# A hybrid RWKV-7 and band-attention encoder on one core: two slots of small steps in a row, then eight steps of large products

## The chip, the cores and the metric

The kernel runs on one core of a Trainium2 chip. A core has five engines that run their own queues in parallel and meet through semaphores: TensorE (PE, matrix products into PSUM), VectorE (DVE) and ScalarE (ACT) for elementwise work, GpSimd (POOL), and SyncE (SP), which here only issues DMAs. Each engine takes its instructions in the order in which they stand in its queue. The metric is the device time of one execution in microseconds (us), as the median of several runs; lower is better.

## What is computed

The reference is a trunk of two layers on 256 tokens of width 2048. Layer 0 mixes over time with RWKV-7 and then has a squared-ReLU MLP; layer 1 attends in bands of chunks and has another such MLP. The change touches only the time mixing, which the reference writes as a recurrence over the tokens for each of 32 heads of size 64:

```python
r = xr @ w_r
k = xk @ w_k
v = xv @ w_v
...
def step(S, inp):
    r_t, w_t, k_t, v_t, kk_t, a_t = inp
    sa = jnp.einsum('bhvk,bhk->bhv', S, -kk_t)
    S = (S * w_t[:, :, None, :] + sa[..., None] * (kk_t * a_t)[:, :, None, :]
         + v_t[..., None] * k_t[:, :, None, :])
    y = jnp.einsum('bhvk,bhk->bhv', S, r_t)
    return S, y
...
y = y.reshape(B, T, D).astype(h.dtype) * g
return y @ w_o
```

## The kernel before

Everything is held feature by token: 16 tiles of 128 features by 256 tokens. A large product is made of two parts for accuracy. The weight and the activation are each split into a high and a low half in a rounded 32-bit format (`halves` for weights: ACT casts a 128x1024 tile to `wH` in line 378, DVE subtracts to get `wL` in line 381; there are three buffers of each). One step over a tile of 128 inputs (one "kt") is two matmuls, line 412 (wH by both halves of the activation, 512 columns) and line 413 (wL by the high half, 256 columns). A projected tile takes 16 such kt. One pair of `wH` and `wL` covers eight kt.

The time mixing works on 16 pairs of heads (128 features each), one `Pair` object for each. The scan over the tokens is turned into four chunks of 64 tokens. A pair goes through 36 small steps, written as a generator that yields after each:

- `early`, steps 0 to 7: decay, learning rate, normalised key, all elementwise but for a few matmuls (lines 127 and 128 at step 0, the head sums of line 115 at steps 2 and 7, line 105 at step 6). DVE's line 154 at step 3 is the reader of the head sums of step 2.
- `invert`, steps 8 to 19: a triangular inverse for all chunks at once. Step 8 multiplies keys (line 105 into `gr`), ACT copies the parts `da` and `co`, POOL masks them. Step 9 is 16 small transposes by matmul. Steps 10 to 19 are five levels of two: the even one multiplies `tt` by `al` or `co` (line 111) and ACT copies the product to `xs` (lines 243 and 248); the odd one multiplies `u` by `xs` (line 111 again), DVE adds it to `u` (line 254, at the last level line 258 as well) and transposes `u` to `tt` (line 239). The odd step of a level cannot start before ACT has copied `xs`.
- `late`, steps 20 to 35: the four chunks one after the other, three steps each (lines 280 to 307; ACT copies `g` and `sa`, DVE makes the state `zs`), then the normalisation (the head sums of line 115 at step 33, ACT lines 318 and 319, DVE line 320) and the output gate (two matmuls in line 324 at step 35).

The scratch PSUM of the small steps (`psm`, tile `ms`) has two buffers that are handed out in turn, so a third user waits until the reader of the first is through.

The loop over slots (line 871) interleaves the pairs. Pair j starts at slot 8(j+1) and takes one step in each slot, so in the steady part four or five pairs are alive at once, eight steps apart. In every slot the small steps are issued first (inverting pairs, then late ones, then early ones), and after them the large products ("dense"): up to slot 127 two yields of `proj_steps`, that is four kt of the key or receptance projection of the pair that starts next; from slot 128 to slot 163, when all projections are done, the first part of the output projection (`out_steps`, 44 yields of two kt spread evenly over the 36 slots). `issue_after(last)` keeps PE's instructions of a block behind the last one recorded before. In three of four slots from slot 16 on, `ada()` adds one tile of another product, which DVE does by itself (line 454).

The order on PE is thus small steps, four kt, small steps, four kt, and so on. The order on the other engines is chosen by a scheduler from the recorded instructions; they do not follow `issue_after`. A period below is eight slots: one new pair, 32 kt.

Of the kernel before, what the change touches and what calls it, by code (L numbers as in the profile page):

```python
# [24 lines left out]
NPAIR = D // P  # L25
# [304 lines left out]
class Body:  # L330
# [299 lines left out]
    def layer_a(self, st, sp):  # L630
        nc, tc, d = self.nc, self.tc, self.d
# [5 lines left out]
        with ExitStack() as s1:  # L637
# [123 lines left out]
            for n in range(KT):  # L761
# [12 lines left out]
                first, last = n == 0, n == KT - 1  # L774
# [40 lines left out]
        with ExitStack() as s1:  # L815
            pw = self.pw = s1.enter_context(tc.tile_pool(name="pw", bufs=1, reuse_waits="tile"))
            pp = self.pp = sp.enter_context(tc.tile_pool(name="ps_b", bufs=1, space=bass.MemoryType.PSUM,
                                                         reuse_waits="tile"))
            self.psm = lambda: pp.tile([P, 512], F32, tag="ms", bufs=2, name="ms")
            e01 = [pw.tile([P, 4, C + 1], F32, name=f"e01_{i}") for i in range(2)]  # L820
            self.uf = [pw.tile([P, 4, C], F32, name=f"uf_{i}") for i in range(2)]
            for e, u in zip(e01, self.uf):
                nc.vector.memset(e[:, :, 0:1], 1.0)
                nc.gpsimd.memset(u, 0.0)

            pairs = [Pair(self, j, v[:, j, :], tw, ta, tg, e01[j % 2]) for j in range(NPAIR)]

            def proj_steps(pr):
                for dst, hl in (("k", xk), ("r", xr)):
                    w = self.wnext  # L830
                    src = next(weights, None)
                    self.wnext = None if src is None else self.weight(src)
                    ps = pp.tile([P, 2, T], F32, tag="pj", bufs=2, name="pj")
                    for kt in range(KT):
                        self.proj2(ps, w, lambda kt: hl[:, kt, :, 0:T], (kt, kt + 1))
                        if dst == "r" and kt == 1:
                            pr.lw = pw.tile([96, 2, P], F32, tag="lw", bufs=1, name="lw")
                            nc.sync.dma_start(out=pr.lw, in_=d["lora2"][pr.j, :96, 0:2])
                        if kt % 2 == 1:
                            if kt == KT - 1:  # L840
                                t = pw.tile([P, T], F32, tag=dst, bufs=2, name=dst)
                                nc.scalar.copy(t, ps[:, 0, :])
                                nc.vector.tensor_tensor(out=t, in0=ps[:, 1, :], in1=t, op=ALU.add)
                                setattr(pr, dst, t)
                            yield

            def out_steps():

                for n in range(8):
                    self.split(self.y_hl, n, v[:, n, :])  # L850
                sums, todo = self.o_ps, [(n, 0, HK) for n in range(8)] + [(n, HK, KT - 2) for n in range(4)]
                for n, lo, hi in todo:
                    if n % 2 == 0 and lo == 0:
                        tag = ("pj", "pj", "gr", "iv")[n // 2]
                        ps = pp.tile([P, 2 * T], F32, tag=tag, bufs=1 + (tag == "pj"), name="o")
                        sums.append(ps.rearrange("p (i t) -> p i t", i=2))
                    if lo == HK and n == 0:
                        assert all(p.done for p in pairs[:KT - 2])
                        for j in range(HK, KT - 2):
                            self.split(self.y_hl, j, v[:, j, :])  # L860
                    w = self.weight_part(d["w_o"][n], lo, hi)
                    for kt in range(lo, hi, 2):
                        self.proj(sums[n // 2][:, n % 2, :], w, lambda kt: self.y_hl[:, kt, :, 0:T],
                                  (kt, kt + 2), n % 2 == 0, False)
                        yield

            self.o_ps = []
            S, OUTS = self.SLOTS, 44
            inverts = range(Pair.EARLY, Pair.EARLY + Pair.INVERT)
            outs, done, n_out = None, 0, 0  # L870
            for slot in range(S * NPAIR + Pair.STEPS):
                live = []
                for j, pr in enumerate(pairs):
                    at = slot - S * (j + 1)
                    if 0 <= at < Pair.STEPS:
                        if at == 0:
                            pr.gen = pr.steps()
                        live.append((0 if at in inverts else 1 + (at < Pair.EARLY), -at, pr))
                        pr.done = at == Pair.STEPS - 1
                last = self.last_pe()  # L880
                for _, _, pr in sorted(live, key=lambda x: x[:2]):
                    with tc.issue_after(last):
                        next(pr.gen)
                    last = self.last_pe()
                if slot < S * NPAIR:
                    if slot % S == 0:
                        dense = proj_steps(pairs[slot // S])
                    todo = 16 // S
                else:
                    if outs is None:  # L890
                        self.y_hl = self.new_hl()
                        outs = dense = out_steps()
                    todo = OUTS * (slot + 1 - S * NPAIR) // Pair.STEPS - n_out
                    n_out += todo
                with tc.issue_after(last):
                    for _ in range(todo):
                        next(dense, None)
                if slot >= 2 * S and slot % 4 < 3:
                    self.ada()
            self.fin(HK)  # L900
# [306 lines left out]
```

## Time and profile before

| what | value |
|---|---|
| median of 3 runs (lowest, highest) | 2672.63 us (2672.55, 2673.03) |
| the profiled execution | 2673.81 us, of which its span is 2672.0 us |
| busy share of the span | PE 97%, PE weight loads 83%, DVE 79%, ACT 50%, POOL 8% |
| instructions | PE 23690 matmuls, DVE 3109, ACT 2432, POOL 320 |
| first projected key tile to last, of 16 (DVE line 843) | 216.8 us to 621.4 us |
| start of the last projected receptance tile's sum | 633.1 us |
| mean granted TensorE clock | 0.994 of full speed |

The page gives each engine's busy time; a row of a timeline gives the start in us, the duration, the engine, the line, what is written and what is read, and how many instructions were merged into it (for the small matmuls two for each line of the kernel that issues one). A bracket at the end of a row gives the idle time of the engine before it and the instruction whose end released it. The duration of a matmul contains its way through the array, so that successive matmuls overlap in these rows: what a matmul costs PE is the distance between starts. The time mixing's slots lie between about 209 and 715 us of the span; the two MLPs and the attention follow.

### The profile page before, as it was taken

To read this page: it belongs to the slowest core of one execution; us is meant where nothing else is said; L and a number is where in the kernel's file an instruction comes from. 1 tells how busy PE (TensorE), PEld (TensorE's weight loads), DVE (VectorE), ACT (ScalarE), POOL (GpSimd) and SP (SyncE) were. 2 spreads that over 40 slices of the span, in tenths; PEclk is the share of its full clock that TensorE was granted. 3 is DMA by queue.
4 is the path that set the end of the run, shared out by engine and by line. 5 is a ranking of instruction groups with operands and counts; after the bars stand their busy time and mean duration, and the time that the engine had idled before them with its cause. 6 is when DMAs were issued, how large, how long until landed. Compare 5 with 4: busy or idle time off the path is not lost. (4 is left out here: it accounts for less than half of the span.)

```text
span 2672.0 us, 58365 instructions
## 1 busy us (share of the span) xinstructions
PE 2600.1 (97%) x23690; PEld 2225.4 (83%) x23690; DVE 2101.0 (79%) x3109; ACT 1343.9 (50%) x2432; POOL 209.7 (8%) x320
## 2 busy tenths in 40 slices
PE   6999999999999999999999999999999999999997
PEld 3777788788899888888888998877898888888886
DVE  5778888889789888888888898899887556555555
ACT  3345555555456445355365554565564463453554
POOL 0001322332110000000000100000100000000002
PEclk9999999999999999999999999999999999999999
DMA  9966556565768888899898679887766555555553
GB/s 337 314 236 211 192 173 210 189 206 195 245 240 304 324 309 321 322 324 331 320 328 294 238 240 325 324 274 259 264 216 237 186 187 188 189 186 185 189 189 119
DMA packets 217390, 662.64 MB, mean 248 GB/s; under 512 B 21408, under 2 KB 68896, under 8 KB 217120
## 3 DMA queue, kind: packets, MB, share of 16 engines
q1 hardware_dynamic: 215056, 656.36, 71.1%
q8 instruction: 186, 3.05, 0.5%
q10 hardware_dynamic: 2064, 2.54, 0.3%
q14 instruction: 84, 0.69, 0.1%
HBM read 656.72 MB, written 2.10 MB: 247 GB/s over the span
## 5 line engine op out<-in xcount | busy, mean ns | idle before, releaser
L381 DVE TENSOR_TENSOR wL<-raw,wH 128x1024 fp32r<-128x1024 f32 x772 | 940.9, 1220 | 342.6 <-ACT wH L378 337.8
L378 ACT CAST wH<-raw 128x1024 fp32r<-128x1024 f32 x772 | 805.5, 1045 | 801.2 <-PE pj L412 646.0
L412 PE MATMUL pj<-aHL,wH 128*128 128x512 f32 x3328 | 1201.9, 403 | 2.0 <-DVE x L927 1.1
L413 PE MATMUL pj<-aHL,wL 128*128 128x256 f32 x3328 | 936.3, 281 | 0.0
L412 PEld LDWEIGHTS pj<-aHL,wH 128*128 128x128 f32 x3328 | 629.5, 189 | 154.1 <-issue 9.2
L412 PE MATMUL pj<-hHL,wH 128*128 128x512 f32 x2048 | 724.6, 399 | 0.0
L413 PEld LDWEIGHTS pj<-aHL,wL 128*128 128x128 f32 x3328 | 629.7, 189 | 2.6 <-issue 0.8
L413 PE MATMUL pj<-hHL,wL 128*128 128x256 f32 x2048 | 574.7, 281 | 0.0
L412 PEld LDWEIGHTS pj<-hHL,wH 128*128 128x128 f32 x2048 | 384.8, 188 | 95.7 <-DVE hHL L973 0.2
L413 PEld LDWEIGHTS pj<-hHL,wL 128*128 128x128 f32 x2048 | 387.0, 189 | 0.1
L454 DVE SCALAR_TENSOR_TENSOR acc<-rada,ct,acc 128x1024 f32<-128x1024 f32 x256 | 327.5, 1279 | 8.4 <-DMA rada<-w_ada 7.5
L518 POOL TENSOR_TENSOR ss<-ss,sq 128x256 f32<-128x256 f32 x56 | 54.5, 974 | 1590.8 <-ACT sq L517 1590.5
L998 DVE SCALAR_TENSOR_TENSOR x<-pj,mod,x 128x256 f32<-128x256 f32 x256 | 123.3, 482 | 59.5 <-PE pj L413 55.7
L454 DVE SCALAR_TENSOR_TENSOR acc<-raw,ct,acc 128x1024 f32<-128x1024 f32 x104 | 136.4, 1312 | 15.5 <-DMA raw<-w_ada 15.4
L401 PE MATMUL pj<-aHL,wH 128*128 128x258 f32 x384 | 109.0, 284 | 0.0
L402 PE MATMUL pj<-aHL,wH 128*128 128x258 f32 x384 | 109.0, 284 | 0.0
L970 ACT ACTIVATE t<-t 128x256 f32<-128x256 f32 x112 | 46.8, 418 | 122.6 <-DVE t L942 122.6
L403 PE MATMUL pj<-aHL,wL 128*128 128x258 f32 x384 | 108.0, 281 | 0.0
L403 PEld LDWEIGHTS pj<-aHL,wL 128*128 128x128 f32 x384 | 73.2, 191 | 0.2
L402 PEld LDWEIGHTS pj<-aHL,wH 128*128 128x128 f32 x384 | 72.6, 189 | 0.1
L401 PEld LDWEIGHTS pj<-aHL,wH 128*128 128x128 f32 x384 | 72.2, 188 | 0.2
L972 ACT ACTIVATE t<-t 128x256 f32<-128x256 f32 x128 | 53.4, 417 | 3.4
(244 smaller groups left out, 2812.3 us busy)
## 6 DMA issues: line engine op xcount, KB each, us to landing
raw<-w_up SPq DMA_DIRECT2D x256, 512.0 KB, 4.1
raw<-w_down SPq DMA_DIRECT2D x256, 512.0 KB, 4.1
rada<-w_ada SPq DMA_DIRECT2D x209, 512.0 KB, 5.7
raw<-w_ada SPq DMA_DIRECT2D x111, 512.0 KB, 4.4
rawa<-w_ada SPq DMA_DIRECT2D x64, 512.0 KB, 6.8
rada<-w_ada_kv SPq DMA_DIRECT2D x64, 512.0 KB, 6.6
raw<-w_k SPq DMA_DIRECT2D x32, 512.0 KB, 4.2
raw<-w_r SPq DMA_DIRECT2D x32, 512.0 KB, 4.5
```

The lines of the kernel that those rows point to most:

```text
L378: nc.scalar.copy(Hf, raw)
L381: eng.tensor_tensor(out=Lf, in0=raw, in1=Hf, op=ALU.subtract)
L401: nc.tensor.matmul(ps, H[:, i, :], a(kt)[:, 0, :], start=(first and kt == 0), stop=False)
L402: nc.tensor.matmul(ps, H[:, i, :], a(kt)[:, 1, :], start=False, stop=False)
L403: ins = nc.tensor.matmul(ps, L[:, i, :], a(kt)[:, 0, :], start=False, stop=(last and kt == KT - 1))
L412: nc.tensor.matmul(ps, H[:, i, :], a(kt), start=(kt == 0), stop=False)
L413: ins = nc.tensor.matmul(ps[:, 0, :], L[:, i, :], a(kt)[:, 0, :], start=False, stop=(kt == KT - 1))
L454: nc.vector.scalar_tensor_tensor(out=self.acc, in0=raw, scalar=ck, in1=self.acc, op0=ALU.mult, op1=ALU.add)
L518: (eng or nc.gpsimd).tensor_tensor(out=self.ss, in0=self.ss, in1=sq, op=ALU.add)
L970: nc.scalar.activation(t, t, AF.Relu)
L972: nc.scalar.activation(t, t, AF.Square)
L998: nc.vector.scalar_tensor_tensor(out=x, in0=ps[:, i, :], scalar=self.mods[(layer, 5)][:, n:n + 1], in1=x, op0=ALU.mult, op1=ALU.add)
```

## The change

The large products are issued in odd slots alone, and twice as many of them. Even slots issue only small steps. On PE the small steps of slots 2m and 2m+1 therefore follow directly on one another, and then come eight kt (in the last 36 slots the yields of two slots) instead of four. The projection of a pair is begun one slot later and ends in the same slot as before; the number of instructions does not change.

```diff
@@ -882,19 +882,20 @@
                     with tc.issue_after(last):
                         next(pr.gen)
                     last = self.last_pe()
-                if slot < S * NPAIR:
-                    if slot % S == 0:
-                        dense = proj_steps(pairs[slot // S])
-                    todo = 16 // S
-                else:
-                    if outs is None:
-                        self.y_hl = self.new_hl()
-                        outs = dense = out_steps()
-                    todo = OUTS * (slot + 1 - S * NPAIR) // Pair.STEPS - n_out
-                    n_out += todo
-                with tc.issue_after(last):
-                    for _ in range(todo):
-                        next(dense, None)
+                if slot % 2:
+                    if slot < S * NPAIR:
+                        if slot % S == 1:
+                            dense = proj_steps(pairs[slot // S])
+                        todo = 32 // S
+                    else:
+                        if outs is None:
+                            self.y_hl = self.new_hl()
+                            outs = dense = out_steps()
+                        todo = OUTS * (slot + 1 - S * NPAIR) // Pair.STEPS - n_out
+                        n_out += todo
+                    with tc.issue_after(last):
+                        for _ in range(todo):
+                            next(dense, None)
                 if slot >= 2 * S and slot % 4 < 3:
                     self.ada()
             self.fin(HK)
```

## The prediction

> **What bounds the kernel now.** I read the page first, then the busy time in stretches of the time mixing, then PE's waits in its steady part, then single rows of the timeline. The page:
>
> ```profile
> span 2672.0 us, 58365 instructions
> PE 2600.1 (97%) x23690; PEld 2225.4 (83%) x23690; DVE 2101.0 (79%) x3109; ACT 1343.9 (50%) x2432; POOL 209.7 (8%) x320
> ```
>
> The change stays inside slots 0 to 163. Its steady stretch and its last slots (start and end, length, then busy time and count of PE, weight loads, DVE, ACT, POOL, the granted clock, the DMA share, GB/s):
>
> ```profile
> 330.00:640.00 310.00, 305.30 (x6379) 250.40 (x6374) 269.08 (x514) 168.79 (x482) 88.07 (x120) 1.00 0.59 192
> 640.00:715.00 75.00, 70.96 (x1423) 61.28 (x1405) 63.56 (x109) 30.02 (x85) 10.45 (x17) 1.00 0.69 230
> ```
>
> PE is busy 98% of the steady stretch, DVE 87%, ACT 54%. All that PE waits for there (us in total, times, the longest):
>
> ```profile
> PE ms L324 <- DVE s L154: 1.9, 5, 0.8
> PE iv L111 <- DVE tt L239: 1.5, 2, 1.2
> PE lt L280 <- DVE zs L307: 0.7, 2, 0.3
> ```
>
> That is 4.1 us in 310. PE's own order sets the pace, and nearly everything that it needs from ACT and DVE arrives while it works through four kt. So the change is worth what PE saves by switching less often, minus the waits which that cover hid.
>
> **What is saved.** The starts of the rows count. One slot of the steady part:
>
> ```profile
> 422.11 0.28 PE L302 MATMUL lt<-vp,bk 64*64 64x64 f32 x4
> 422.22 0.28 PE L280 MATMUL lt<-vp,mk 64*64 64x64 f32 x4
> 422.44 0.50 PE L412 MATMUL pj<-aHL,wH 128*128 128x512 f32 x1
> ...
> 422.89 0.40 PE L412 MATMUL pj<-aHL,wH 128*128 128x512 f32 x1
> ...
> 423.25 0.40 PE L412 MATMUL pj<-aHL,wH 128*128 128x512 f32 x1
> ...
> 424.04 0.45 PE L111 MATMUL iv<-u,xs 32*32 32x32 f32 x32
> ```
>
> A kt in full flow takes 423.25 - 422.89 = 0.36 us, the block of four 424.04 - 422.44 = 1.60. So a block carries 1.60 - 4 x 0.36 = 0.16 us of switching, and 0.11 more ahead of it (0.22 from the last small group to the first large matmul, against 0.11 from one group to the next). Where two slots join, one such switch goes, and a change from one kind of small matmul to another comes, whose cost no row shows by itself. It lies between nothing and the 0.16 + 0.11 of a switch to a large product and back, so the saving is 0 to 0.27 us; I take 0.2, since groups of small matmuls follow at 0.11 us and differ less from each other than from a large one. Four joins a period: 0.8 us (0 to 1.1).
>
> **What is uncovered.** A period is eight slots. In the order of the built program the even and the odd slot of each join stand on PE as the diff says (now and then one group of line 105 trades places with line 111), and PE starts nothing past a matmul that waits. I go through the four joins by the slots of a period.
>
> *Slots 2 and 3, first wait.* At step 18 PE multiplies into `ms`, ACT copies it to `xs` (line 248), and step 19 needs that.
>
> ```profile
> 442.38 0.34 PE L111 MATMUL ms<-tt,co 32*32 32x32 f32 x10
> ...
> 443.75 0.58 PE L412 MATMUL pj<-aHL,wH 128*128 128x512 f32 x1
> ...
> 445.42 0.34 PE L111 MATMUL ms<-u,xs 32*32 32x32 f32 x10
> ...
> 446.19 1.13 PE L324 MATMUL ms<-tg,lg 128*128 128x256 f32 x4
> ```
>
> ```profile
> 443.51 1.03 ACT L378 CAST wH<-raw 128x1024 fp32r<-128x1024 f32 x1
> 444.57 0.53 ACT L248 COPY xs<-ms 32x128 f32<-32x128 f32 x2
> ...
> 613.97 0.53 ACT L248 COPY xs<-ms 32x128 f32<-32x128 f32 x2
> ```
>
> ```profile
> 613.48 0.35 PE L111 MATMUL ms<-tt,co 32*32 32x32 f32 x10
> ```
>
> Without the four kt PE is ready for step 19 at 443.75; the copy ends at 444.57 + 0.53 = 445.10. That is a wait of 1.4 us, because ACT comes late out of the work of slots 0 and 1 and has a weight cast first. The built program keeps that order on ACT. Six periods on, ACT is in time: its copy ends 613.97 + 0.53 - 613.48 = 1.0 us after step 18 begins, and 443.75 - 442.38 = 1.37 us are there. So 0 to 1.4 us. I take 0.8, nearer the middle than the dear end, since a longer period also gives ACT and DVE time to catch up.
>
> *Slots 2 and 3, second wait.* Line 324 at step 35 takes over the `ms` buffer that line 154 on DVE reads. Before, DVE does line 154 ahead of lines 258 and 254. In the changed program it stands behind them, and these two read what PE makes just before line 324. DVE in that order, as it happened once before:
>
> ```profile
> 643.80 0.57 DVE L258 COPY uf<-ms 32x128 f32<-32x128 f32 x2
> 644.40 0.29 DVE L254 TENSOR_TENSOR u<-u,iv 128x128 f32<-128x128 f32 x1
> 644.61 0.48 DVE L325 SCALAR_TENSOR_TENSOR sl<-v,vecs,sl 128x256 f32<-128x256 f32 x1
> 645.00 0.42 DVE L154 TENSOR_SCALAR s<-ms 128x256 f32<-128x256 f32 x1
> ```
>
> This takes 1.62 us, or 1.62 - 0.39 = 1.23 where line 325 isn't between (7 of 11 periods; where the twelfth stands, the order was so already). From line 154 to line 324 there is little more:
>
> ```profile
> 417.82 0.41 DVE L154 TENSOR_SCALAR s<-ms 128x256 f32<-128x256 f32 x1
> 418.28 1.13 PE L324 MATMUL ms<-tg,lg 128*128 128x256 f32 x4 [0.75 <-DVE s L154]
> ```
>
> 0.05 us, and here PE already waited 0.75. Step 19's first product ends no sooner than 445.42 + 0.34, my estimate with its interleaved rest is 445.9; the chain then ends at 445.9 + 1.23 + 0.05 = 447.2 (447.6 with line 325) where PE got to line 324 at 446.19. The wait is 1.0 us (1.4), 1.13 on the mean; 1.9 / 12 = 0.16 of it was there before. That leaves 1.0 for each of 11 periods (0.7 if DVE is let in early, 1.25). Queued behind line 324 on PE are line 287 and the eight kt. ACT waits for 287 with `sa`, DVE for 324 with `v`, and on SP the next load of `lg`, whose one buffer line 324 reads, holds up the weight loads queued behind it.
>
> *Slots 4 and 5.* ACT copies `xs` at step 12, behind a weight cast and the sum of `k`:
>
> ```profile
> 422.42 0.27 ACT L243 COPY xs<-iv 128x128 f32<-128x128 f32 x1
> ```
>
> It ends at 422.69; PE would be ready for it at 422.44, so 0.3 us. The states `zs` come behind a weight's `wL` on DVE and can add the 0.3 of the third wait above: 0.4 (0.2 to 0.6).
>
> *Slots 6 and 7* have the same two copies, but with a longer row of matmuls between: 0.1 (0 to 0.3).
>
> *Slots 0 and 1.* The head sums of step 33 need the `ms` buffer that line 132 reads:
>
> ```profile
> 437.24 0.86 DVE L132 TENSOR_SCALAR s<-ms,vecs 128x256 f32<-128x256 f32 x2
> 439.40 0.70 PE L115 MATMUL ms<-sq,csts 128*128 128x256 f32 x2
> ```
>
> Line 132 ends at 438.10; without the block PE is there at 439.40 - 1.60 = 437.80. 0.3 us at most, and I take 0.2, since DVE's order varies here.
>
> **The sum.** The same row of step 18 stands at 442.38 and, six periods on, at 613.48, so a period lasts 28.5 us. Slots 32 to 127 are 12 periods with four or five pairs alive. Each changes by -0.8 + 0.8 + 0.4 + 0.1 + 0.2 = +0.7 us, and 11 of them by 1.0 more: 8.4 + 11 = +19 us. In the three periods ahead and the 36 slots behind, 12 + 18 joins save 0.2 each, 6 us; there are fewer pairs to fill a wait and less large work to hide it (two yields hardly cover a trip to ACT and back), so I put 0.1 to 0.45 us on each join, 3 to 13: +2 (-3 to +7). The weights' DMAs are issued one slot later, but PE holds up to three pairs of halves and each serves eight kt, two slots: nothing; if that cover went, a late tile would cost the 1.03 us of its cast and about as much on DVE, once. Sum: +21 us, to the profiled execution's 2673.81, of which 2672.0 is the span and 1.8 lies around it. Its time is 1.2 above the median, so 2694. With all bounds at one side: 12 x (-1.1 + 0.2) + 11 x 0.7 - 3 = -6 us, and 12 x (1.4 + 0.6 + 0.3 + 0.3) + 11 x 1.25 + 7 = +52 us.
>
> **The rivals.** *The cover wasn't needed.* If ACT and DVE, which are idle 46% and 13% of the stretch, run ahead as in the row at 613.97, and the scheduler's places cost nothing, only savings stay: 30 + 48 joins by 0.2 are -16 us, 2657. For it: waits of 4.1 us now. Against it: copies that end 1.4 us too late for the joined order, and line 154's new place. It decides if PE's waits in the steady stretch stay below 12 x 0.8 = 10 us.
>
> *Even.* The waits come and are about as large as the savings, 2673. [...]
>
> *The clock.* Once, early in the time mixing, PE stood still for over 3 us, and the clock fell:
>
> ```profile
> 280.00:285.00 5.00, 1.62 (x52) 1.59 (x54) 4.85 (x8) 0.45 (x2) 2.07 (x2) 0.80 0.61 204
> 285.00:290.00 5.00, 5.00 (x67) 4.00 (x63) 1.94 (x4) 0.37 (x1) 0.00 (x0) 0.52 0.67 206
> ```
>
> Two waits of 1.4 us follow closely in slots 2 and 3; should they trip it each period, 5 us at 0.52 lose 2.4 us, 12 times: +29 on the sum, 2723. In the last 75 us PE was idle for 4.0 us in pieces and the clock stayed at 1.00. [...]
>
> **How the numbers follow.** 0.2% is 5.3 us, about what a measurement of this kernel can tell from no change. My forecast, slower by 6 to 40 us with 2694 likeliest, 0.69; cover not needed 0.13, faster; even 0.12; clock, or waits near their upper bounds, 0.06. Faster 0.13, same 0.12, slower 0.75. The range leaves out the savings alone and the clock: 2668 to 2712.
>
> **What would show it.** In the profile after: line 324 waiting for line 154 some 11 times for about 1 us; line 111 waiting for ACT's lines 248 and 243; PE's busy share of the steady stretch at 92 to 94%, with blocks of eight kt of about 3.0 us; the stretch about 20 us longer, all else unmoved. If line 324 doesn't wait, or the copies of `xs` are there, my prices are wrong; if PE is as busy as before, the mechanism is.

## The result, and the profile after

| | before | after |
|---|---|---|
| median (lowest to highest, runs) | 2672.59 us (2672.17 to 2673.03, 4) | 2705.89 us (2701.84 to 2707.61, 4) |
| the profiled execution | 2673.81 us | 2707.07 us |
| last receptance sum (DVE line 843) | 633.1 us | 668.1 us |

The changed kernel is slower by 33.3 us; the ratio is 1.012, with a 95% interval of 1.0108 to 1.0132. The last row places the loss: 668.1 - 633.1 = 35 us are lost by slot 127, and the 36 slots behind give 2 back.

The page of the changed kernel, span and busy times:

```profile
span 2705.3 us, 58379 instructions
PE 2614.6 (97%) x23690; PEld 2236.6 (83%) x23690; DVE 2099.3 (78%) x3109; ACT 1345.8 (50%) x2432; POOL 203.9 (8%) x320
```

PE's share of the whole is unchanged, so the page alone hides the loss. The stretches of the time mixing show it (columns as before: PE, weight loads, DVE, ACT, POOL, granted clock, DMA share, GB/s):

```profile
330.00:640.00 310.00, 288.99 (x5629) 235.99 (x5630) 235.01 (x452) 145.39 (x414) 70.77 (x103) 0.94 0.53 171
640.00:715.00 75.00, 69.26 (x1635) 58.57 (x1636) 64.34 (x127) 38.20 (x114) 15.91 (x28) 0.97 0.57 183
```

In the first, PE does 5629 matmuls in place of 6379, is busy 93% in place of 98%, and does them at a granted clock of 0.94 in place of 1.00. Two things were lost, time and speed. The first shows in PE's waits in the same 310 us (us in total, times, longest):

```profile
PE ms L115 <- DVE s L132: 8.2, 5, 2.3
PE ms L324 <- PE iv L111: 4.8, 9, 0.6
PE ms L111 <- ACT xs L248: 4.4, 3, 1.8
PE lt L280 <- DVE zs L305: 1.8, 2, 1.5
PE ms L324 <- issue: 1.2, 1, 1.2
PE ms L115 <- issue: 0.7, 1, 0.7
```

These are 21.1 us against 4.1. The largest is at line 115 (slots 0 and 1). One case of it, in the timeline of DVE and PE:

```profile
349.59 2.61 DVE L454 SCALAR_TENSOR_TENSOR acc<-raw,ct,acc 128x1024 f32<-128x1024 f32 x2 [3.23 <-DMA raw<-w_ada]
...
352.78 1.22 DVE L381 TENSOR_TENSOR wL<-raw,wH 128x1024 fp32r<-128x1024 f32 x1
353.91 0.87 DVE L132 TENSOR_SCALAR s<-ms,vecs 128x256 f32<-128x256 f32 x2
...
354.84 0.82 PE L115 MATMUL ms<-sq,csts 128*128 128x256 f32 x2 [2.10 <-DVE s L132]
```

Read it upward. PE waits 2.10 us for line 132; DVE did nothing slow in line 132, but reached it late, because it had stood for 3.23 us ahead of the first row, at line 454, until a weight of the other product landed, and everything behind line 454 in DVE's queue waited with it. The kernel before has such stands too:

```profile
DVE acc L454 <- DMA raw<-w_ada: 13.0, 11, 2.0
```

After the change:

```profile
DVE acc L454 <- DMA raw<-w_ada: 18.5, 11, 3.4
```

There are eleven in both (us in total, times, longest). Before, four kt between the small steps of slots 0 and 1 ran meanwhile.

The second loss, the speed, in three stretches of 3.41 us that follow on one another around the same wait:

```profile
351.86:355.28 3.42, 1.31 (x32) 1.03 (x28) 3.42 (x8) 2.20 (x8) 0.90 (x2) 1.00 0.83 228
355.28:358.69 3.41, 3.41 (x27) 2.73 (x26) 3.41 (x7) 3.06 (x9) 3.02 (x5) 0.50 0.76 257
358.69:362.10 3.41, 3.41 (x70) 2.75 (x68) 1.22 (x4) 1.82 (x5) 1.79 (x3) 1.00 0.46 160
```

In the first, PE is busy for 1.31 us; in the second it is busy throughout, at half the clock, and gets 27 matmuls done; in the third the clock is back. The record of the clock has eight such dips between 330 and 640 us, eleven stretches of 3.41 us in all, and none there before. The blocks of eight kt, 3.0 us long at full clock, last 11.7 us longer there in all.

The joins of slots 2 and 3, at their first wait:

```profile
424.18 1.03 ACT L378 CAST wH<-raw 128x1024 fp32r<-128x1024 f32 x1
425.24 0.53 ACT L248 COPY xs<-ms 32x128 f32<-32x128 f32 x2
425.82 0.44 PE L111 MATMUL ms<-u,xs 32*32 32x32 f32 x16 [1.79 <-ACT xs L248]
```

and at their second, in another period:

```profile
362.90 0.57 DVE L258 COPY uf<-ms 32x128 f32<-32x128 f32 x2
...
363.57 1.10 PE L324 MATMUL ms<-tg,lg 128*128 128x256 f32 x4 [0.50 <-PE iv L111]
363.71 0.42 DVE L154 TENSOR_SCALAR s<-ms 128x256 f32<-128x256 f32 x1
```

Line 324 starts when line 258 is through (362.90 + 0.57 = 363.47), and before line 154 begins. So its buffer is the one that line 258 reads, not line 154's; the bracket names the last matmul of PE, which had been done before that.

### The profile page after: what moved, and what is told of

Same layout as the page of the kernel before. It is cut to its first block, busy times and chain, and to the rows that moved or that the text cites. A ratio compares the mean times of both kernels' runs of the same rounds, so it can differ in the third digit from the quotient of the medians.

```text
span 2705.3 us, 58379 instructions
## 1 busy us (share of the span) xinstructions
PE 2614.6 (97%) x23690; PEld 2236.6 (83%) x23690; DVE 2099.3 (78%) x3109; ACT 1345.8 (50%) x2432; POOL 203.9 (8%) x320
## 4 chain that ended last, share of the span: by engine, by line
PE 81%; DVE 8%; issue 4%; DMA 4%; ACT 2%; POOL 1%; SPq 0%; DVEq 0%; POOLq 0%; ACTq 0%
PE pj L412 44%; PE pj L413 22%; DVE acc L454 2%; DMA raw<-w_ada 2%; PE pj L402 2%; PE pj L401 2%; PE pj L403 2%; DVE wL L381 2%; ACT wH L378 1%; PE iv L111 1%; PE ms L324 1%; PE ms L115 1%; DVE mix L732 0%; DMA rada<-w_ada 0%; PE pT L1103 0%
```

## The experiments

The first set joins only some of the pairs of slots, with all else as before.

```diff
-                with tc.issue_after(last):
-                    for _ in range(todo):
-                        next(dense, None)
+                owed += todo
+                if slot % S not in JOIN:
+                    with tc.issue_after(last):
+                        for _ in range(owed):
+                            next(dense, None)
+                    owed = 0
```

`JOIN = (0,)`:

> Only slots 0 and 1 of each eight are joined; all other slots keep their four kt. Theory 1 (waits uncovered at the join, and clock dips that these waits set off): the head sums of line 115 wait for line 132 on DVE in about half of the periods, up to 2.3 us, and some of these waits are followed by a stretch of 3.4 us at half clock; 2677 to 2686 us. Theory 2 (the whole loss comes from slots 2 and 3, which disturb the rest): no wait at line 115, 2670 to 2674 us.

`JOIN = (2,)`:

> Only slots 2 and 3 are joined. Theory 1: line 111 waits for ACT's line 248 in about half of the periods, line 324 waits 0.5 us in each, clock dips follow the longest waits; 2682 to 2692 us, the largest of the three parts. Rival (the parts need each other, since only a kernel late everywhere is late here): at most 2677 us.

`JOIN = (4, 6)`:

> Only slots 4 and 5, and 6 and 7, are joined. Theory 1: their small steps take 0.2 to 0.3 us more and the large block 0.2 us less, which cancels; few waits, no clock dip; 2670 to 2677 us. If joining saved 0.2 us each as the prediction has it: 30 joins or so, 2664 to 2668 us.

| kernel | median us (lowest to highest, runs) | ratio to before, 95% interval |
|---|---|---|
| e1, slots 0/1 | 2681.01 (2677.58 to 2684.09, 6) | 1.0030 (1.0018 to 1.0042) |
| e2, slots 2/3 | 2704.13 (2702.70 to 2709.42, 4) | 1.0122 (1.0107 to 1.0137) |
| e3, slots 4/5 and 6/7 | 2672.34 (2670.33 to 2679.51, 10) | 1.0005 (0.9996 to 1.0015) |
| before, same chip | 2672.9 (2668.94 to 2675.55, 15) | |

Two joins out of four (e3) change nothing: what they save and what they uncover come out even. The join of slots 0/1 (e1) lies in the expected range, but not by the expected way: PE's waits at line 115 in the steady stretch are 0.9 and 1.0 us at most, 3.4 us in all, and the clock doesn't dip there; where its 8 us go isn't shown in full. The join of slots 2/3 alone costs 31 us, as much as the whole change, where 2682 to 2692 was expected. Its timeline shows how:

```profile
519.69 1.28 DVE L454 SCALAR_TENSOR_TENSOR acc<-raw,ct,acc 128x1024 f32<-128x1024 f32 x1 [1.59 <-DMA raw<-w_ada]
520.89 1.22 DVE L381 TENSOR_TENSOR wL<-raw,wH 128x1024 fp32r<-128x1024 f32 x1
522.03 0.57 DVE L258 COPY uf<-ms 32x128 f32<-32x128 f32 x2
...
522.70 2.05 PE L324 MATMUL ms<-tg,lg 128*128 128x256 f32 x4 [3.09 <-issue]
```

It is the stand at line 454 again. Here it falls ahead of line 258, and PE waits 3.09 us at line 324, one of three such waits (7.9 us in all); the next stretch of 3.41 us has a granted clock of 0.51. In the whole change the same stands fall mostly on line 115. In e3 DVE stands at line 454 for 21.4 us of the steady stretch, longer than in the changed kernel, and nothing is lost. So the joins don't add up (8 + 31 + 0 against 33): what a stand costs depends on which uncovered product is behind it.

The next kernel is the changed one with extra large matmuls by a zero weight, five ahead of line 115 at step 33 and three ahead of line 111 at step 19, which add nothing to any result but keep PE busy where it waits.

```diff
+                    for _ in range(n):
+                        nc.tensor.matmul(self.sink[0:16], self.zero, xk[:, 0, :, 0:T], start=start, stop=start)
...
+            if l == 5:
+                b.fill(3, False)
...
+        b.fill(5, True)
```

> The changed kernel with idle work added: products with a zero weight, 128x16 by 512 columns, added into the running sum, five ahead of line 115 at step 33 (1.2 us) and three ahead of step 19 (0.7 us) in each period. If the clock dips cost time of their own (theory 1): at most 3 dips in the time mixing in place of 9, blocks of eight kt at 3.0 us throughout, 2698 to 2708 us, since the added work costs about 11 us where no wait hides it and the dips gave 13. If the dips fall into time that is lost anyway (rival): 2712 to 2720 us. If zero weights don't count as work for the clock: dips as before.

It took 2698.66 us (2693.59 to 2701.56, 4 runs; ratio 1.0102, interval 1.0085 to 1.0118), 7 us less than the changed kernel with more work on PE. (That is little: the intervals of the two ratios overlap, though all four runs lie below all four of the changed kernel.) Its steady stretch, and its group of added matmuls there:

```profile
330.00:640.00 310.00, 301.68 (x6005) 239.33 (x6007) 248.26 (x473) 154.39 (x435) 77.94 (x111) 1.00 0.55 175
```

```profile
L834 PE MATMUL pj<-aHL,zero 128*16 128x512 f32 x80 | 23.9, 420 | 0.0
```

The clock is 1.00. In this stretch PE now loses 23.9 us to the added matmuls and 8.3 to waits, 32.2 in all against 21.0 in the changed kernel, and still gets 5925 matmuls of the program done against 5629: the half clock costs time of its own, apart from the wait ahead of it. How much is not told by it, since DVE's stands at line 454 are shorter here too (10.5 us against 18.5).

Next, the tiles of the other product (line 454) are taken out of the time mixing, in both kernels; they are made up later.

```diff
-                if slot >= 2 * S and slot % 4 < 3:
-                    self.ada()
```

> The kernel before, without the tiles of the other product (line 454) in the slots of the time mixing: they are made up after it, in one piece, so the whole is longer. It is the base for e6. In e2 and in the changed kernel, DVE stood in the tile's line for 1.6 to 3.2 us until its weight had landed, and the products that PE waited for were queued behind. All theories: the time mixing itself a little shorter than before (DVE has 1.3 us less to do in six of eight slots), PE's waits in its steady part below 4 us, the whole later by the made-up tiles, which I don't put a number on.

> The changed kernel, with the same taken out; read against e5. Theory 1 (the loss is mostly DVE held by these tiles, which the four kt between the small steps used to cover, and the dips of the clock that follow): e6 minus e5 is 2 to 12 us instead of 33, PE never waits 2 us at line 115 or 324, and two half-clock stretches or fewer stand in the steady part. Theory 2 (the chains through ACT and DVE are themselves too long for the joined order, whatever else DVE has to do): e6 minus e5 stays at 22 to 40 us.

The whole took 2786.39 us (2785.09 to 2790.62, 4 runs) and 2804.31 us (2801.42 to 2806.00, 4 runs). The difference is 17.9 us, between the two theories: about half of the loss is there without these tiles. (In the profiled executions it is 15.4 us; by the last receptance sum, at 614.35 and 627.94 us, 13.6 of them are lost, where the whole change loses 35 by then.) The profile without the tiles is clean. The steady stretch of the kernel before:

```profile
330.00:640.00 310.00, 310.00 (x6398) 255.86 (x6397) 207.24 (x458) 172.80 (x498) 82.04 (x123) 1.00 0.27 86
```

and of the changed kernel, with all that PE waits for in it:

```profile
330.00:640.00 310.00, 301.34 (x6106) 245.97 (x6106) 200.39 (x446) 167.79 (x483) 80.63 (x119) 1.00 0.27 83
```

```profile
PE ms L324 <- PE iv L111: 5.4, 10, 0.5
PE ms L111 <- ACT xs L248: 2.9, 10, 0.3
```

Without the tiles PE of the kernel before never waits at all. In the changed kernel two waits stand in each period, 0.54 and 0.29 us, both in slots 2 and 3; line 115 doesn't wait, and the clock is full. The starts of step 18, nine periods apart, give the periods' length. Before, without the tiles:

```profile
345.03 0.25 PE L111 MATMUL ms<-tt,co 32*32 32x32 f32 x4
...
593.01 0.22 PE L111 MATMUL ms<-tt,co 32*32 32x32 f32 x2
```

After, without the tiles, with a block of eight kt:

```profile
347.62 0.25 PE L111 MATMUL ms<-tt,co 32*32 32x32 f32 x4
...
373.26 0.50 PE L412 MATMUL pj<-aHL,wH 128*128 128x512 f32 x1
...
376.25 0.31 PE L111 MATMUL ms<-tt,co 32*32 32x32 f32 x8
...
605.49 0.28 PE L111 MATMUL ms<-tt,co 32*32 32x32 f32 x6
```

That is (593.01 - 345.03) / 9 = 27.55 us and (605.49 - 347.62) / 9 = 28.65 us: the bare change costs 1.10 us a period. Where it is lost shows when the period is cut behind every second block of large products in e5, and behind every block in e6, at the start of the first small matmul (means of nine periods, us; the periods hardly differ):

| slots | e5 | e6 | difference |
|---|---|---|---|
| 2 and 3 | 6.60 | 7.59 | +0.99 |
| 4 and 5 | 6.20 | 6.37 | +0.17 |
| 6 and 7 | 6.33 | 6.30 | -0.03 |
| 0 and 1 | 8.43 | 8.39 | -0.04 |

So the loss is that of the waits. In slots 2 and 3 they are longer than the idle time says: in flow the next matmul starts before the one ahead has ended, by 0.07 us at this place:

```profile
348.32 0.46 PE L111 MATMUL iv<-u,xs 32*32 32x32 f32 x23
348.71 1.13 PE L324 MATMUL ms<-tg,lg 128*128 128x256 f32 x4
```

In e5 line 324 starts at 348.71, while line 111 ends at 348.32 + 0.46 = 348.78. In e6 it starts 0.54 us after that end, 0.61 later than in flow; with 0.29 + 0.07 at line 111 that is 0.97 of the 0.99. In slots 4 and 5, line 111 waits for ACT's copy of line 243, and PE's weight load with it (0.26 us at 356.74 in e6).

Where no wait stands, a join saves next to nothing, 0.03 and 0.04 us. The large products do gain: the block of eight takes 376.25 - 373.26 = 2.99 us against twice 1.60. The small steps lose nearly as much where they meet. Line 128 ends slot 0; before, without the tiles, and after:

```profile
366.21 0.59 PE L128 MATMUL ms<-ta,lw 96*128 96x256 f32 x2
366.45 0.59 PE L412 MATMUL pj<-aHL,wH 128*128 128x512 f32 x1
```

```profile
369.92 0.59 PE L128 MATMUL ms<-ta,lw 96*128 96x256 f32 x2
370.44 0.45 PE L111 MATMUL iv<-u,xs 32*32 32x32 f32 x32
```

From line 128 to a large product 0.24 us pass, to a small matmul 0.52. In slots 6 and 7 the joint itself is short (0.15 us behind line 105), but line 280 follows line 296 after 0.24 us in e6 and 0.11 in e5.

Then the load of each tile is issued one call earlier, in both kernels.

```diff
                     self.ada()
+                    self.ada_load()
```

> The kernel before, with the load of each such tile issued one call earlier than the line that uses it, into one more of the six raw buffers. Theory 1: DVE no longer stands there for a load; PE hardly waited for it before, so 2666 to 2676 us. Theory 2, or if the raw buffers are what is short (the tile holds one longer, and the weights come later): 2673 to 2690.

> The changed kernel with the same earlier load. Theory 1: the waits of 2 to 3 us at lines 115 and 324 go, and most of the half-clock stretches with them: 2676 to 2692 us. Theory 2: 2700 to 2712, as the changed kernel. If a buffer is short, line 454 waits as often as before, and the time is as in theory 2 or above it.

2680.46 us (2673.26 to 2682.93, 10 runs; ratio 1.0030, 1.0021 to 1.0040) and 2711.49 us (2707.53 to 2717.93, 4 runs; 1.0151, 1.0133 to 1.0169). Both are slower, and both miss theory 1's range. In the changed kernel DVE stands at line 454 for 21.4 us in the steady stretch, no less than the 18.5 without the earlier load. In the kernel before the stands fall from 13.0 to 7.4 us, and the last receptance sum comes at 632.0 us, no later than the 633.1 of before: its loss lies behind that. For the changed kernel the early issue is no cure; whether the loads lack a buffer or the DMA queue's turn wasn't separated.

The next three leave the number of tiles and move the calls: only after odd slots (that is, in the changed kernel, behind a block of eight kt), or three each after slots 3 and 5 (`self.ada(3)`).

```diff
-                if slot >= 2 * S and slot % 4 < 3:
-                    self.ada()
+                if slot >= 2 * S and slot % 2:
+                    self.ada(2 if slot % 4 == 1 else 1)
```

> The kernel before with the tiles of the other product called only after odd slots, two and one by turns in place of one in three of four slots; the same tiles in all. The base for e10. Nothing of the joins is in it: 2668 to 2680 us by each theory.

> The changed kernel with the same: no tile is called between two slots that are joined, each stands behind a block of eight kt. What is known: e6 minus e5 is 18 us (28.65 against 27.55 us a period) without the tiles, 33 with them. Theory 1 (the other 15 us are DVE standing for a tile's weight just where the block of four kt is gone, and the half-clock stretches that such a wait brings): the wait at line 115 falls from 8.2 us to below 4 in the steady part, half-clock stretches there from nine to four or fewer, and the time to 2683 to 2697 us. Theory 3 (it is the tile's work on DVE and its load on the DMA queue, wherever they stand): 2700 to 2712 us, with the waits at another line.

> The changed kernel with three tiles called after slot 3 and three after slot 5 of each eight, none from slot 6 to slot 2 of the next eight, so that the joins of slots 0/1 and 2/3, which can wait least, stand far from them. Theory 1: no wait over 1 us at line 115, 2680 to 2695 us, if the three at once don't stop line 307 or 305 of slots 4/5 as long instead. Theory 3: 2700 to 2712 us or, with three loads at once, above it.

2675.41 us (2672.12 to 2680.10, 10 runs; 1.0008, 0.9999 to 1.0018) for the base, 2701.04 us (2698.80 to 2703.35, 4 runs; 1.0107, 1.0090 to 1.0124) and 2695.37 us (2693.39 to 2706.77, 4 runs; 1.0096, 1.0075 to 1.0118). The waits at line 115, first with the calls after odd slots, then with three each after slots 3 and 5:

```profile
PE ms L115 <- DVE s L132: 7.0, 4, 3.0
```

```profile
PE ms L115 <- DVE s L132: 7.0, 5, 2.3
```

A miss for theory 1 as I had put it: the wait stays, and e10's time lies in the range of theory 3. Moving the calls in the program didn't move DVE's stands away from the joins; DVE's order is the scheduler's. The half-clock stretches in the steady part fell from eleven to eight and five, which goes with the 5 and 10 us by which the medians lie below the changed kernel's; the intervals of the ratios still overlap with its 1.0108 to 1.0132.

The last kernel keeps DVE's work on the tiles and takes away the loads alone; it leaves out this part of the other product.

```diff
+            raw = None
+            if not (self.dry and kt):
+                raw = self.raw(w[kt * P:(kt + 1) * P, half * n_:(half + 1) * n_], ada=True)
...
-            nc.vector.scalar_tensor_tensor(out=self.acc, in0=raw, scalar=ck, in1=self.acc, op0=ALU.mult, op1=ALU.add)
+            nc.vector.scalar_tensor_tensor(out=self.acc, in0=self.acc if raw is None else raw, scalar=ck, in1=self.acc, op0=ALU.mult, op1=ALU.add)
```

> The changed kernel in which, inside the time mixing, 15 of 16 tiles of the other product are not loaded: DVE does the same instruction of the same size on its running sum in place of the weight (this part of the product is left out, and those loads with it). So DVE's work is that of the changed kernel, and only the standing for a load, and the loads on the DMA queue, are gone. Base: 31.6 us a period with the loads, 28.65 without the tiles (e6); 27.55 and 28.54 for the kernel before. Theory 1 (DVE standing for a weight to land): 28.5 to 29.4 us a period, no wait of over 1 us at line 115, no half-clock stretch or one in the steady part, 2670 to 2685 us. Theory 3 (the 1.3 us that each tile takes on DVE): 30 us a period or more, the wait at line 115 stays at 4 us or more, 2690 to 2706 us.

2684.49 us (2683.32 to 2687.46, 6 runs; ratio 1.0041, 1.0026 to 1.0055), 21.4 us less than the changed kernel. All of PE's waits above 1 us in total in its steady stretch:

```profile
PE ms L111 <- ACT xs L248: 5.5, 8, 1.1
PE ms L324 <- PE iv L111: 4.8, 9, 0.6
PE ms L324 <- issue: 1.1, 1, 1.1
```

The wait at line 115 is gone without a trace, with DVE's work as it was: DVE stood for the loads, and that was the cause, as theory 1 has it. The loads' traffic went with them (the DMA share of the steady stretch is 0.28 in place of 0.53), but none of PE's waits in the changed kernel goes back to the load of a projection's weight. Three dips of the clock remain (five stretches, where theory 1 had one at most), behind waits of 1.1 us for `xs`. The period is (625.82 - 354.14) / 9 = 30.2 us by these rows, above the 29.4 that I had as upper end and where theory 3 had its lower one; periods without a dip last 29.1 to 29.9:

```profile
354.14 0.34 PE L111 MATMUL ms<-tt,co 32*32 32x32 f32 x10
...
625.82 0.34 PE L111 MATMUL ms<-tt,co 32*32 32x32 f32 x10
```

The kernel before would gain from the loads' absence as well, which wasn't run. I take its gain to be at most what taking out the tiles altogether gave it: its period is (613.48 - 356.63) / 9 = 28.54 us, so 28.54 - 27.55 = 0.99 us in each of 12 periods, or 12 us. So by this estimate the stands for the loads and the dips that follow them make 9 to 21 of the 33 us; the difference of e6 - e5 to the whole, 33.3 - 17.9 = 15.4, lies inside.

No kernel here beats the one before; e3 equals it.

## Why the prediction came out as it did

The forecast was slower by about 21 us, from uncovered waits; it is slower by 33, inside the range. The direction, and the mechanism that PE's order loses its cover, held. Without the other product's tiles, the four joins cost what the sum said to within 0.1 us each, but for slots 2 and 3, which cost 0.99 where it had 1.6 in 11 of 12 periods. By the last receptance sum that makes 13.6 us where the sum had 19 for its 12 periods. The other 21 of the 35 us come with the tiles, by a stand of DVE that the sum had at next to nothing and by the half clock, which it left to a rival. That the time still lies in the range is partly luck.

*Held.* Line 111 waits for line 248 behind a weight cast: 0.3 us in a quiet period (e6), up to 1.8 in the changed kernel, and 4.4 / 10 = 0.4 us a period, inside 0 to 1.4, below my 0.8. PE's busy share of the steady stretch is 93%, as said, and an undisturbed block of eight kt takes 3.0 us. The joins of slots 4 to 7 cost nothing to speak of (e3; +0.17 and -0.03 us a period by e5 and e6), where I had +0.4 and +0.1 for waits and twice -0.2 for the savings. The 36 slots at the end gave 2 us back, where both ends together were put at +2.

*"So the saving is 0 to 0.27 us; I take 0.2."* The range holds, the 0.2 doesn't: the joins without a wait save 0.03 and 0.04 us. The step took the joint between two rows of small steps to be nearly as cheap as the 0.11 us between groups of small matmuls, and held that no row shows such a change by itself. A row does. In the kernel before, line 115, 256 columns wide as line 128 is, starts at 439.40, and line 291 behind it at 440.03:

```profile
439.40 0.70 PE L115 MATMUL ms<-sq,csts 128*128 128x256 f32 x2
440.03 0.33 PE L291 MATMUL lt<-mk,vp 64*64 64x64 f32 x4
```

That is 0.63 us, and in e5 a large product follows line 115 after 0.34 (346.05 to 346.39). Four joins in 12 periods at 0.16 less are about 8 us on the sum.

*Slots 2 and 3, second wait.* The wait is there in nearly every period, but it is 0.5 us of idle time (0.61 from start to start in e6), not 1.0, and for line 258, not line 154. I had taken the buffer's reader from the order before; by the rows at 362.90 to 363.71 it is another one. The term was too large by 0.4 to 0.5 us, in 11 periods some 5 us.

*Slots 0 and 1, "0.3 us at most".* This was the step that failed most. It took one row in which DVE was on time (line 132 at 437.24) as the rule. The bound had to come from DVE's worst lateness: line 454 stood eleven times for a load in those 310 us, up to 2.0 us, but no PE wait showed it because the four kt covered it. Uncovered, it is 8.2 us at line 115 in ten periods (and with only slots 2/3 joined, up to 3.09 us at line 324). e12 shows that the load is what DVE stands for.

*The clock, a rival with a small chance.* It came in part. That two waits of 1.4 us which follow closely in slots 2 and 3 could do it, each period, was the forecast's assumption; in fact dips came behind single waits of about 1 to 2 us, eight times in these 310 us, behind line 115 and behind line 111 three times each. Eleven half-clock stretches can cost by estimate at most 11 x 3.41 x 0.5 = 19 us; the 11.7 us by which the large blocks are longer is what can be seen directly. e4 shows that there is a cost apart from the waits, without giving it a size.

*The rivals "cover wasn't needed" and "even".* The first fell at its own point of decision: PE's waits are 21 us, above 10. Its picture, ACT and DVE in time for the joined order, comes nearest where the other product's tiles are away (e6), and even there the change loses 1.1 us a period. "Even" had waits and savings cancel; the waits are 21 us in the steady stretch, a join without a wait saves 0.03 to 0.04, and the time moved by 33 us. DVE did not set the pace of the kernel before: e5 takes 269.08 / 310 x 28.54 - 207.24 / 310 x 27.55 = 6.4 us a period off DVE, a quarter of its work, and the period falls by 0.99 only. PE is then busy 310.00 of 310 us and waits for nothing, with the weight loads at 255.86 (83%).

So the structural part (17.9 us by e6 - e5, 13.6 of it by slot 127) is near the 21 predicted, with less wait and next to no saving. What was missing is the load's landing on DVE and the half clock, the other 15.4. How these 15.4 divide between the two stays open.

## What to carry to other kernels

Before a cover is taken away, look not at the idle time of the engine that is covered, which shows nothing, but at the longest stand of every engine that feeds it, above all a wait for a DMA that holds up its queue: here DVE's stands at line 454, up to 2.0 us long before, were up to 3.4 us long after, and waits of up to 2.3 us at line 115 appeared. A large product between groups of small ones was worth more here as cover than the 0.03 to 0.04 us that a join without a wait saved. And price a new wait of TensorE by the granted clock as well: here a wait of 1 to 2 us could cost about as much again (3.41 us at half clock, 1.7 us by estimate) in the microseconds after it.

## What the runs showed of the hardware

In each of the 14 traces the dips of the clock start at multiples of 3.413 us from one another (in the changed kernel those at 355.28 and 454.27 us are 29 x 3.413 apart), and between 330 and 640 us they last one or two such windows. I sorted the windows of 330 to 640 us at full clock in all 14 traces by the share in which PE was busy (from the starts and durations of its matmuls), and counted how often the next window had half the clock:

```
PE busy in the window    windows    next one at half clock
under 50%                16         16
50 to 60%                 9          6
60 to 70%                23          6
70 to 75%                16          5
75% or more            1156          0
```

No dip between 330 and 640 us came behind a window that was idle throughout: the longest gap inside the window was 0.6 to 2.5 us before a dip. A little over a quarter of a window idle (0.9 us) was the least that was followed by a dip, and more than half a window idle (1.7 us) was followed by one in all 16 cases. Between 50 and 75% the share alone doesn't tell. In the changed kernel a wait of 1.63 us that ended at 492.27 lay across a border of two windows (491.8), PE was busy for 66 and 70% of them, and no dip followed. These are counts from 310 us of each of these kernels; they don't show what sets the clock.

The other surprise is the joint of two kinds of small matmuls. A block of eight kt takes 0.2 us less than two of four, and yet a join without a wait saves only 0.03 to 0.04 us. At slots 0 and 1 a small matmul starts 0.52 us behind line 128 (256 columns), where a large product starts 0.24 us behind it. The rows show the cost, not its reason.
